# Two layers of a transformer block on one core: the first feed-forward groups as two pairs 512 columns wide, matmuls ordered by width, smaller first weight pieces

## The chip, the core and the metric

The kernel runs on one core of a Trainium2 chip. The time is the device time of one execution in microseconds (us); lower is better. Matrix products run on TensorE (PE), whose weight loads have a row of their own in the profile (PEld). VectorE (DVE), ScalarE (ACT) and GpSimd (POOL) do the elementwise work; SyncE (SP) issues nearly all DMAs.

## The reference

Two layers over 256 tokens of 1024 features. A mixer with three branches (a gated linear attention, a gated MLP over chunks, a softmax attention) ends in a residual and a layer norm. Then comes the part that the change is mostly about:

```python
x = layer_norm(DEEPNORM_ALPHA * x + mix, ln1_g[l], ln1_b[l])
ff = jnp.square(jax.nn.relu(x @ w_ff1[l])) @ w_ff2[l]      # 1024 -> 4096 -> 1024
x = layer_norm(DEEPNORM_ALPHA * x + ff, ln2_g[l], ln2_b[l])
```

All arrays are float32.

## The kernel before

**Precision.** TensorE multiplies in the type fp32r. Each float32 operand is split into a part `hi` (a cast on ScalarE) and a rest `lo` (a subtraction on VectorE); a product is the sum of hi·hi, hi·lo and lo·hi. The activations lie transposed, as `hi` and `lo` of 1024 features by 256 tokens, the two side by side so that `both` is one operand of 512 columns.

**Weights.** They come from memory in pieces of 1024 columns by 128 partitions (512 KB) into four raw buffers. `split_hi` makes `whi` (line 115) and `split_lo` makes `wlo` (line 120); each has 9 buffers (`SPLIT_BUFS`). The raw buffer is free once `wlo` is made, and then the next DMA is issued.

**Units.** The program is a list of units, each a stretch of matmuls (`pe`) that uses one or a few weight pieces, with work behind it (`post`). A planner at the end of the function fixes at which unit each piece is split: at most `LEAD` = 7 units ahead of its use, at most two pieces in one unit, and not before the piece that held the same buffer was used for the last time. The main loop then does the following for each unit, in this order, and each engine executes its instructions in the order in which they are written:

```python
        advance()      # next step of every generator in `side`
        splits(i)
        u.pe()
        if u.post:
            u.post()
```

Work that has to wait a while is put into `side` as a generator; each `yield` in it lets one more unit's matmuls go ahead of it.

**Three forms of matmul.** `acc_s` (line 287) has tokens as the stationary operand and weights as the moving one, 256 or 512 columns wide; its result has tokens on the partitions. `acc_w` (line 263) is the reverse, 256 wide. `acc_wide` (line 275) is the reverse with `both` as the moving operand: for each k one wide matmul (whi by `both`, 512 columns) and one narrow (wlo by `hi`, 256 columns), in turn.

**The feed-forward.** The 4096 hidden features are 16 groups of 256. Groups 3 to 15 are made by `ff1_units` with `acc_wide`: 2 units of 16 matmuls each, and no transpose is needed. The first three groups, the head, are made by `acc_s` for the first 128 tokens and then for the second, so that they can begin before the layer norm of the second 128 tokens is done: 6 units of 24 matmuls of 256 columns. Behind each, ScalarE does Relu (line 910) and Square (911) on the 128x256 result, TensorE transposes it in two pieces (919), and ScalarE and VectorE make `h` hi and lo (922, 923). The generator `tr` has two yields between Square and the transposes. `ff2_units(j)` multiplies group j by the second matrix, two units of 12 matmuls of 512 columns each, and alternates with `ff1_units(j + 3)`; the last three groups go into `out_units` (6 pieces).

**The layer norm** (`residual_norm`) of the second 128 tokens transposes its result (line 214, tile pT) at the start of the third unit after its own last one; line 216 casts it to `hi` and line 217 makes `lo`.

**The start.** `first_units` makes two products of 512 columns each (pSv, pSgv) over k = 0 to 7. Its pieces are 512 columns for k = 0 (two of them) and 1024 columns for k = 1 to 7; x comes in four pieces (k = 0; 1; 2 and 3; 4 to 7) that are split in `split_x` (lines 983, 984).

Of the kernel before, what the change touches and what calls it, by code (L numbers as in the profile page):

```python
# [9 lines left out]
F32 = mybir.dt.float32  # L10
# [4 lines left out]
OP = mybir.AluOpType  # L15
# [21 lines left out]
LEAD = 7  # L37
# [17 lines left out]
def block_kernel(ctx, tc, ins, out):  # L55
# [209 lines left out]
    def acc_wide(o, p, x, cs, k0, start, stop):  # L265


        hi, both = x[0], x[2]
        n = p.shape[0]
        for i in range(n):  # L270
            k = k0 + i
            tr = [(o, p.hi[:, i, cs], both[:, k, :]), (o[:, :256], p.lo[:, i, cs], hi[:, k, :])]
            last = stop and i == n - 1
            for j, (d, w, a) in enumerate(tr[::-1] if last else tr):
                nc.tensor.matmul(d, w, a, start=start and i == 0 and j == 0, stop=last and j == 1)  # L275
# [27 lines left out]
    def build_layer(l, xT):  # L303
# [285 lines left out]
        def first_units():  # L589

            blocks = [(0, piece(w_in[:, 0:1, C_V:C_V + 512], 1, 512)), (0, piece(w_in[:, 0:1, C_GV:C_GV + 512], 1, 512))]
            blocks += [(k, piece(w_in[:, k:k + 1, C_V:C_V + 1024], 1, 1024)) for k in range(1, 8)]
            heads = {0: 0, 2: 1, 3: 2, 5: 3}
            for n, (k, p) in enumerate(blocks):
# [3 lines left out]
                def pe(k=k, p=p, n=n):  # L598
                    for i, nm in enumerate(("v", "gv")):
                        if n < 2 and i != n:  # L600
                            continue
                        c0 = i * 512 if n > 1 else 0
                        for t in range(NT):
                            if k == 0:
                                st["ps_" + nm, t] = pbank("ps", "pS" + nm)
                            o, ts, cs = st["ps_" + nm, t], slice(t * 128, (t + 1) * 128), slice(c0, c0 + 512)
                            nc.tensor.matmul(o, xT()[0][:, k, ts], p.hi[:, 0, cs], start=k == 0, stop=False)
                            nc.tensor.matmul(o, xT()[1][:, k, ts], p.hi[:, 0, cs], start=False, stop=False)
                    for i, nm in enumerate(("v", "gv")):
                        if n < 2 and i != n:  # L610
                            continue
                        c0 = i * 512 if n > 1 else 0
# [279 lines left out]
        NS = 3  # L892
# [6 lines left out]
        fb = [w_pieces(wf1, j * 256, 256) for j in range(NS)]  # L899
        for t in range(NT):  # L900
            for j in range(NS):
                def pe(j=j, t=t):
                    p = st["pf", j, t] = pbank("pw", "pF")
                    for k in range(8):
                        acc_s(p[:, :256], fb[j][k // 4], k % 4, x1T(), k, t, slice(0, 256), k == 0, k == 7)

                def post(j=j, t=t):
                    def tr():
                        r = sbt("SP" if j % 2 else "PT", 384, "fr", bufs=2)[:, :256]
                        nc.scalar.activation(r, st["pf", j, t][:, :256], AF.Relu)  # L910
                        nc.scalar.activation(r, r, AF.Square)
                        yield
                        yield
                        if t == 0:
                            new_h(j)
                        hi, lo = st["h", j]
                        p = pbank("pw", "pFT")
                        for i in range(2):
                            nc.tensor.transpose(p[:, i * 128:(i + 1) * 128], r[:, i * 128:(i + 1) * 128], ident)
                        ts = slice(t * 128, (t + 1) * 128)  # L920
                        pv = v3(p[:, :256], 2)
                        nc.scalar.copy(hi[:, :, ts], pv)
                        nc.vector.tensor_tensor(lo[:, :, ts], pv, hi[:, :, ts].bitcast(F32), op=OP.subtract)
# [67 lines left out]
    units[3].start = sts[0]["params"]  # L991
# [23 lines left out]
    for n, p in enumerate(pieces):  # L1015
        free = max(q.last for q in pieces[:n - SPLIT_BUFS + 1]) + 1 if n >= SPLIT_BUFS else -LEAD
        s = max(prev + 1, free, p.first - (LEAD if n > 8 else 1))
# [5 lines left out]
        lo_at.setdefault(max(min(s + 1, p.first), s, -1) if n > 8 else max(s, -1), []).append(p)  # L1023
# [31 lines left out]
    for n, c in ((0, 0), (2, 1), (3, 2), (5, 3)):  # L1055
        load_more(n)
        load_xT(c)
# [56 lines left out]
```

## Time and profile before

| | us |
|---|---|
| median of 3 runs (lowest, highest) | 872.27 (872.25, 872.44) |
| the profiled execution, whole | 872.83 |
| its span, first to last instruction | 871.1 |
| TensorE busy | 860.2 (99% of the span) |
| VectorE busy | 617.7 (71%) |
| ScalarE busy | 468.0 (54%) |
| TensorE's share of the chain that ended last | 92% |

The span is the time from the first instruction to the last. The chain that ended last is followed back from the last instruction, at each step to what it waited for. A busy TensorE is not one at its peak: ends of matmuls are modelled and overlap, so rates are read from starts and from counts in a stretch.

### The profile page before, as it was taken

Reading aid. Unit: us, or ns where it says so; the run is one execution under the profiler, and the core shown is the slowest. Engines: PE = TensorE matmul, PEld = TensorE weight load, DVE = VectorE, ACT = ScalarE, POOL = GpSimd, SP = SyncE. Lnnn points to the kernel's source line nnn. Section 1 sums busy time; section 2 is a strip of 40 time slices with the busy share of each in tenths; the row PEclk is TensorE's granted clock in tenths of the full one; section 3 lists DMA queues with packets and bytes.
Section 4 is the critical chain, followed back from the end, with each engine's and each line's share of the span. In section 5 each row is a group of like instructions: output and inputs, shape, how many; then the busy total and the mean of one; then the engine's idle time right before and its main releaser. Section 6 shows DMA issues by size and latency. Waiting matters only on the chain.

```text
span 871.1 us, 13093 instructions
## 1 busy us (share of the span) xinstructions
PE 860.2 (99%) x5020; PEld 751.4 (86%) x5020; DVE 617.7 (71%) x949; ACT 468.0 (54%) x768; POOL 59.5 (7%) x73
## 2 busy tenths in 40 slices
PE   9999999999999999999999999999999999999996
PEld 7898887889989888888889898878898988888885
DVE  6779798666796666666777767958667856666665
ACT  6657663567445544445454756645744555444440
POOL 0010000102400000000000100010042000000001
PEclk9999999999999999999999999999999999999999
DMA  9577665346566655556655765544467465555531
GB/s 324 201 220 214 198 218 151 115 148 191 189 198 212 217 190 186 190 191 209 216 172 170 218 198 165 171 120 146 151 217 229 147 224 193 193 194 194 194 121 48
DMA packets 118718, 162.10 MB, mean 186 GB/s; under 512 B 5472, under 2 KB 100480, under 8 KB 118656
## 3 DMA queue, kind: packets, MB, share of 16 engines
q1 hardware_dynamic: 118512, 161.15, 57.8%
q8 instruction: 39, 0.64, 0.3%
q14 instruction: 23, 0.19, 0.1%
q10 hardware_dynamic: 144, 0.13, 0.0%
HBM read 160.21 MB, written 1.05 MB: 185 GB/s over the span
## 4 chain that ended last, share of the span: by engine, by line
PE 92%; DVE 3%; DMA 2%; ACT 1%; issue 1%; SPq 0%; DVEq 0%; ACTq 0%
PE acc L287 25%; PE pW L275 25%; PE pF L275 17%; PE pB L263 8%; PE pF L287 4%; PE pSmv L287 3%; DVE wlo L120 1%; PE pGG L287 1%; PE pSgv L287 1%; PE pSv L287 1%; PE pkv L457 1%; DMA xraw<-in_xT_dram 1%; DMA inv<-in_rope_inv_dram 1%; PE po L481 1%; PE pT L214 1%
## 5 line engine op out<-in xcount | busy, mean ns | idle before, releaser
L115 ACT CAST whi<-wraw 128x1024 fp32r<-128x1024 f32 (+1 forms) x281 | 283.3, 1039 | 132.2 <-DMA wraw<-in_w_ff_dram 63.2
L120 DVE TENSOR_TENSOR wlo<-wraw,whi 128x1024 fp32r<-128x1024 f32 (+1 forms) x281 | 334.7, 1226 | 18.1 <-ACT whi L115 17.8
L275 PE MATMUL pW<-actT,whi 128*128 128x512 f32 x704 | 248.3, 401 | 0.0
L275 PE MATMUL pW<-actT,wlo 128*128 128x256 f32 x704 | 183.3, 281 | 0.0
L287 PE MATMUL acc<-whi,h 128*128 128x512 f32 x512 | 163.4, 391 | 0.0
L275 PEld LDWEIGHTS pW<-actT,whi 128*128 128x128 f32 x704 | 128.1, 188 | 24.4
L275 PE MATMUL pF<-actT,whi 128*128 128x512 f32 x416 | 146.7, 397 | 0.0
L275 PEld LDWEIGHTS pW<-actT,wlo 128*128 128x128 f32 x704 | 132.9, 189 | 7.3 <-DVE wlo L120 0.2
L287 PEld LDWEIGHTS acc<-whi,h 128*128 128x128 f32 x512 | 96.2, 188 | 19.0
L275 PE MATMUL pF<-actT,wlo 128*128 128x256 f32 x416 | 108.4, 281 | 0.0
L287 PE MATMUL acc<-wlo,h 128*128 128x512 f32 x256 | 99.8, 390 | 0.0
L279 DVE TENSOR_TENSOR fr<-pF,fr 128x256 f32<-128x256 f32 x52 | 21.9, 424 | 102.0 <-ACT fr L278 102.0
L275 PEld LDWEIGHTS pF<-actT,whi 128*128 128x128 f32 x416 | 76.5, 188 | 15.4
L275 PEld LDWEIGHTS pF<-actT,wlo 128*128 128x128 f32 x416 | 78.5, 189 | 4.4
L287 PEld LDWEIGHTS acc<-wlo,h 128*128 128x128 f32 x256 | 48.1, 188 | 10.0
L278 ACT COPY fr<-pF 128x256 f32<-128x256 f32 x52 | 19.1, 372 | 59.4 <-PE pF L275 59.4
L209 POOL TENSOR_TENSOR mvar<-mvar,halfc 128x1 f32<-128x1 f32 x12 | 10.8, 904 | 443.1 <-DVE mvar L208 443.1
L287 PE MATMUL acc<-whi,actT 128*128 128x512 f32 x128 | 40.3, 391 | 0.0
L287 PE MATMUL pF<-whi,actT 128*128 128x256 f32 x192 | 36.6, 287 | 0.0
L279 DVE TENSOR_TENSOR gates<-pW,gates 128x256 f32<-128x256 f32 x48 | 19.5, 421 | 17.8 <-ACT gates L278 17.4
L278 ACT COPY gates<-pW 128x256 f32<-128x256 f32 x48 | 16.9, 370 | 27.3 <-PE pW L275 27.3
L946 ACT CAST h<-fr 128x256 fp32r<-128x256 f32 x52 | 19.3, 407 | 21.5 <-DVE fr L945 21.5
(234 smaller groups left out, 1238.6 us busy)
## 6 DMA issues: line engine op xcount, KB each, us to landing
wraw<-in_w_ff_dram SPq DMA_DIRECT2D x128, 512.0 KB, 4.9
wraw<-in_w_in_dram SPq DMA_DIRECT2D x104, 512.0 KB, 4.3
wraw<-in_w_branch_dram SPq DMA_DIRECT2D x24, 512.0 KB, 4.3
wraw<-in_w_out_dram SPq DMA_DIRECT2D x16, 512.0 KB, 3.3
wearly<-in_w_in_dram SPq DMA_DIRECT2D x7, 512.0 KB, 9.4
wraw<-in_w_in_dram SPq DMA_DIRECT2D x6, 396.0 KB, 4.4
lng<-in_ln_g_dram SPq DMA_DIRECT2D x4, 512.0 KB, 5.4
lnb<-in_ln_b_dram SPq DMA_DIRECT2D x4, 512.0 KB, 7.3
```

The lines of the kernel that those rows point to most:

```text
L115: nc.scalar.copy(p.hi, p.raw)
L120: nc.vector.tensor_tensor(p.lo, p.raw, p.hi.bitcast(F32), op=OP.subtract)
L209: nc.gpsimd.tensor_tensor(dst, dst, half_c.to_broadcast([128, n]) if n > 1 else half_c, op=OP.pow)
L214: nc.tensor.transpose(p[:, k * 128:(k + 1) * 128], src[:, (half * 4 + k) * 128:(half * 4 + k + 1) * 128], ident)
L263: nc.tensor.matmul(o, w, a, start=start and i == 0 and j == 0, stop=stop and i == n - 1 and j == 2)
L275: nc.tensor.matmul(d, w, a, start=start and i == 0 and j == 0, stop=last and j == 1)
L278: nc.scalar.copy(dst, p[:, 256:])
L279: nc.vector.tensor_tensor(dst, p[:, :256], dst, op=OP.add)
L287: nc.tensor.matmul(o, a, w, start=start and j == 0, stop=stop and j == 2)
L457: nc.tensor.matmul(p[:, h * 128:(h + 1) * 128], kT4[rows, t, h, :], v4[rows, t, h, :], start=True, stop=True)
L481: nc.tensor.matmul(p[r, c], at4[:, t, h, r], v4[:, t, h, :], start=first and r.start == 0, stop=True)
L946: nc.scalar.copy(hi[:, i], rr[i])
```

## The change

Three things. **The head** covers four groups instead of three, in two pairs: 4 units of 24 matmuls of 512 columns; Relu and Square are 128x512, four transposes follow each unit, and `tr` has one yield instead of two before them. Its weights come in eight pieces instead of six. Twelve groups instead of 13 are left to `ff1_units`, and the last `out_units` of a layer has 8 pieces instead of 6. **The order in `acc_wide`**: for each unit and result tile first four wide matmuls, then four narrow ones, or the reverse where the sum ends. **The first pieces**: four of 512 columns (k = 0 and 1), then 1024 columns for k = 2 to 7.

```diff
@@ acc_wide
-        for i in range(n):
-            k = k0 + i
-            tr = [(o, p.hi[:, i, cs], both[:, k, :]), (o[:, :256], p.lo[:, i, cs], hi[:, k, :])]
-            last = stop and i == n - 1
-            for j, (d, w, a) in enumerate(tr[::-1] if last else tr):
-                nc.tensor.matmul(d, w, a, start=start and i == 0 and j == 0, stop=last and j == 1)
+        wide = [(o, p.hi[:, i, cs], both[:, k0 + i, :]) for i in range(n)]
+        narrow = [(o[:, :256], p.lo[:, i, cs], hi[:, k0 + i, :]) for i in range(n)]
+        tr = narrow + wide if stop else wide + narrow
+        for j, (d, w, a) in enumerate(tr):
+            nc.tensor.matmul(d, w, a, start=start and j == 0, stop=stop and j == len(tr) - 1)
@@ first_units
-            blocks = [(0, piece(w_in[:, 0:1, C_V:C_V + 512], 1, 512)), (0, piece(w_in[:, 0:1, C_GV:C_GV + 512], 1, 512))]
-            blocks += [(k, piece(w_in[:, k:k + 1, C_V:C_V + 1024], 1, 1024)) for k in range(1, 8)]
-            heads = {0: 0, 2: 1, 3: 2, 5: 3}
+            blocks = [(k, piece(w_in[:, k:k + 1, c:c + 512], 1, 512)) for c in (C_V, C_GV) for k in (0, 1)]
+            blocks += [(k, piece(w_in[:, k:k + 1, C_V:C_V + 1024], 1, 1024)) for k in range(2, 8)]
+            heads = {0: 0, 1: 1, 4: 2, 6: 3}
@@ build_layer, the feed-forward
-        NS = 3
+        NS = 4
...
-        fb = [w_pieces(wf1, j * 256, 256) for j in range(NS)]
+        fb = [w_pieces(wf1, j * 512, 512, 8, 2) for j in range(NS // 2)]
         for t in range(NT):
-            for j in range(NS):
+            for j in range(NS // 2):
                 def pe(j=j, t=t):
                     p = st["pf", j, t] = pbank("pw", "pF")
                     for k in range(8):
-                        acc_s(p[:, :256], fb[j][k // 4], k % 4, x1T(), k, t, slice(0, 256), k == 0, k == 7)
+                        acc_s(p, fb[j][k // 2], k % 2, x1T(), k, t, slice(0, 512), k == 0, k == 7)

                 def post(j=j, t=t):
                     def tr():
-                        r = sbt("SP" if j % 2 else "PT", 384, "fr", bufs=2)[:, :256]
-                        nc.scalar.activation(r, st["pf", j, t][:, :256], AF.Relu)
+                        if t == 0:
+                            st["fr", j] = sbt(("Rk", "Rgg")[j], 1024, "fr")
+                        r = st["fr", j][:, t * 512:(t + 1) * 512]
+                        nc.scalar.activation(r, st["pf", j, t], AF.Relu)
                         nc.scalar.activation(r, r, AF.Square)
                         yield
-                        yield
-                        if t == 0:
-                            new_h(j)
-                        hi, lo = st["h", j]
                         p = pbank("pw", "pFT")
-                        for i in range(2):
+                        for i in range(4):
                             nc.tensor.transpose(p[:, i * 128:(i + 1) * 128], r[:, i * 128:(i + 1) * 128], ident)
                         ts = slice(t * 128, (t + 1) * 128)
-                        pv = v3(p[:, :256], 2)
-                        nc.scalar.copy(hi[:, :, ts], pv)
-                        nc.vector.tensor_tensor(lo[:, :, ts], pv, hi[:, :, ts].bitcast(F32), op=OP.subtract)
+                        pv = v3(p, 4)
+                        for i in range(2):
+                            if t == 0:
+                                new_h(2 * j + i)
+                            hi, lo = st["h", 2 * j + i]
+                            nc.scalar.copy(hi[:, :, ts], pv[:, 2 * i:2 * i + 2])
+                            nc.vector.tensor_tensor(lo[:, :, ts], pv[:, 2 * i:2 * i + 2], hi[:, :, ts].bitcast(F32), op=OP.subtract)
```

How the instructions stand is shown at three places. First TensorE in the first layer's head, behind the second head unit of the kernel before (`pF` are head matmuls, `pFT` the transposes of a head result, `pT` those of the layer norm, `fr` is what Relu and Square wrote, and a name in brackets is an engine that the row waits for):

```order
L287 MATMUL pF<-wlo,actT 128x256
L287 MATMUL pF<-whi,actT 128x256
L214 MATMUL pT<-ident,xr_67 128x128 [waits DVE_49,PE_49]
L214 MATMUL pT<-ident,xr_67 128x128 x3
L214 MATMUL pT<-ident,xr_67 128x128 [waits DVE_49,PE_49]
L214 MATMUL pT<-ident,xr_67 128x128 x3
L919 MATMUL pFT<-ident,fr 128x128 [waits Activation_49]
L919 MATMUL pFT<-ident,fr 128x128
L287 MATMUL pF<-whi,actT 128x256 [waits Activation_49]
```

The changed kernel, behind its first head unit:

```order
L286 MATMUL pF<-wlo,actT 128x512
L286 MATMUL pF<-whi,actT 128x512
L916 MATMUL pFT<-ident,fr 128x128 [waits Activation_49]
L916 MATMUL pFT<-ident,fr 128x128 x3
L286 MATMUL pF<-whi,actT 128x512 [waits PE_49]
L286 MATMUL pF<-wlo,actT 128x512 [waits DVE_49]
```

and behind the second, where the layer norm's transposes stand too:

```order
L286 MATMUL pF<-whi,actT 128x512
L214 MATMUL pT<-ident,xr_67 128x128 [waits PE_49]
L214 MATMUL pT<-ident,xr_67 128x128 x7
L916 MATMUL pFT<-ident,fr 128x128 [waits PE_49,Activation_49]
L916 MATMUL pFT<-ident,fr 128x128 x3
L286 MATMUL pF<-whi,actT 128x512 [waits Activation_49]
```

The two transposes before belong to the first head unit, whose 24 matmuls lie a whole unit back; the four now belong to the unit whose last matmul stands directly above them.

Second, VectorE at the same head, from the end of the second layer norm on; before:

```order
L242 SCALAR_TENSOR_TENSOR xr_67<-xr_67,mvar,lnb 128x512 [waits DVE_49]
L120 TENSOR_TENSOR wlo<-wraw,whi 128x1024 [waits DMAHW0_49,Activation_49]
L120 TENSOR_TENSOR wlo<-wraw,whi 128x1024 [waits DMAHW1_49,Activation_49]
L217 TENSOR_TENSOR actT<-pT,actT 128x4x128 [waits Activation_49] x2
L923 TENSOR_TENSOR h<-pFT,h 128x2x128 [waits Activation_49]
L120 TENSOR_TENSOR wlo<-wraw,whi 128x1024 [waits DMAHW2_49]
```

and in the changed kernel:

```order
L242 SCALAR_TENSOR_TENSOR xr_67<-xr_67,mvar,lnb 128x512 [waits DVE_49]
L924 TENSOR_TENSOR h<-pFT,h 128x2x128 [waits Activation_49] x2
L120 TENSOR_TENSOR wlo<-wraw,whi 128x1024 [waits DMAHW1_49]
L120 TENSOR_TENSOR wlo<-wraw,whi 128x1024 [waits DMAHW2_49]
L120 TENSOR_TENSOR wlo<-wraw,whi 128x1024 [waits DMAHW3_49,Activation_49]
L217 TENSOR_TENSOR actT<-pT,actT 128x4x128 [waits Activation_49] x2
```

The three `wlo` here are those of the second head unit's second, third and fourth piece; they now stand behind the two `h` rows, which come from the transposes at that unit's start.

Third, VectorE at the program's start, before:

```order
L120 TENSOR_TENSOR wlo<-wearly,whi 128x512 [waits DMAHW1_49,Activation_49]
L120 TENSOR_TENSOR wlo<-wearly,whi 128x512 [waits DMAHW2_49,Activation_49]
L984 TENSOR_TENSOR actT<-xraw,actT 128x256 [waits DMAHW3_49,Activation_49]
L984 TENSOR_TENSOR actT<-xraw,actT 128x2x256 [waits DMAHW5_49,Activation_49]
L120 TENSOR_TENSOR wlo<-wearly,whi 128x1024 [waits DMAHW4_49]
```

and in the changed kernel:

```order
L985 TENSOR_TENSOR actT<-xraw,actT 128x256 [waits DMAHW2_49,Activation_49]
L120 TENSOR_TENSOR wlo<-wearly,whi 128x512 [waits DMAHW1_49]
L120 TENSOR_TENSOR wlo<-wearly,whi 128x512 [waits DMAHW3_49,Activation_49]
L120 TENSOR_TENSOR wlo<-wearly,whi 128x512 [waits DMAHW4_49,Activation_49]
L120 TENSOR_TENSOR wlo<-wearly,whi 128x512 [waits DMAHW5_49,Activation_49]
L985 TENSOR_TENSOR actT<-xraw,actT 128x2x256 [waits DMAHW6_49,Activation_49]
```

The `wlo` of k = 1 stood behind the split of x for k = 2 and 3 (128x2x256); both halves of it now stand ahead of that split.

## Rows read from the trace of the kernel before

**Rows 1.** Page of the profile: busy time (part 1), granted TensorE clock (part 2).

```profile
PE 860.2 (99%) x5020; PEld 751.4 (86%) x5020; DVE 617.7 (71%) x949; ACT 468.0 (54%) x768; POOL 59.5 (7%) x73
...
PEclk9999999999999999999999999999999999999999
```

**Rows 2.** Who waited for whom on TensorE, whole span: total, times, longest (us).

```profile
PE pSv L614 <- DVE wlo L120: 1.1, 1, 1.1
```

**Rows 3.** Chain of work that ended last: start us, length us, what, count.

```profile
255.17 5.75 PE pF L287 x48
...
280.15 5.63 PE pF L275 x32
285.78 5.44 PE acc L287 x24
```

**Rows 4.** Timeline of TensorE between two head units: start, length, engine, line, operation.

```profile
264.61 0.28 PE L287 MATMUL pF<-whi,actT 128*128 128x256 f32 x1
264.73 0.38 PE L919 MATMUL pFT<-ident,fr 128*128 128x128 f32 x2
...
265.06 0.28 PE L287 MATMUL pF<-wlo,actT 128*128 128x256 f32 x1
```

**Rows 5.** Timeline of ScalarE behind the unit that ends in rows 4.

```profile
264.93 0.38 ACT L910 ACTIVATE fr<-pF 128x256 f32<-128x256 f32 x1 [0.95 <-PE pF L287]
265.34 0.42 ACT L911 ACTIVATE fr<-fr 128x256 f32<-128x256 f32 x1
```

**Rows 6.** Timeline of ScalarE, one instruction 512 columns wide.

```profile
53.71 0.62 ACT L373 CAST bh<-vs 128x512 fp32r<-128x512 f32 x1 [1.34 <-DVE vs L372]
```

**Rows 7.** Timeline of VectorE at the first head.

```profile
252.93 1.27 DVE L217 TENSOR_TENSOR actT<-pT,actT 128x512 fp32r<-128x512 f32 x2
...
264.26 0.41 DVE L923 TENSOR_TENSOR h<-pFT,h 128x256 fp32r<-128x256 f32 x1
264.59 1.22 DVE L120 TENSOR_TENSOR wlo<-wraw,whi 128x1024 fp32r<-128x1024 f32 x1
```

**Rows 8.** Timeline of TensorE, eight transposes and the second matmul behind them.

```profile
432.11 1.03 PE L214 MATMUL pT<-ident,xr 128*128 128x128 f32 x8
...
433.21 0.39 PE L287 MATMUL acc<-wlo,h 128*128 128x512 f32 x1
```

**Rows 9.** Timeline of TensorE, where two transposes waited.

```profile
74.74 0.39 PE L740 MATMUL plr<-ident,lrs 128*16 128x128 f32 x2 [0.82 <-DVE gates L279]
74.88 0.48 PE L275 MATMUL pW<-actT,whi 128*128 128x512 f32 x1
```

**Rows 10.** Timeline of TensorE, 512-column matmuls after a long run of 256.

```profile
232.33 0.40 PE L287 MATMUL acc<-whi,actT 128*128 128x512 f32 x1
...
233.49 0.62 PE L287 MATMUL acc<-whi,actT 128*128 128x512 f32 x2
```

**Rows 11.** Chain of work that ended last, at the program's start.

```profile
9.99 0.69 DVE actT L984
10.68 1.15 DVE wlo L120
...
11.87 0.73 PE pSv L614 x2
```

**Rows 12.** Timeline of ScalarE at the start: weight cast of the third k.

```profile
10.71 1.04 ACT L115 CAST whi<-wearly 128x1024 fp32r<-128x1024 f32 x1 [0.76 <-DMA wearly<-in_w_in_dram]
```

**Rows 13.** Timeline of TensorE at the start: before and after its first stall.

```profile
5.47 0.63 PE L608 MATMUL pSv<-whi,actT 128*128 128x512 f32 x1
5.89 0.63 PE L607 MATMUL pSv<-whi,actT 128*128 128x512 f32 x1
...
12.43 0.63 PE L614 MATMUL pSgv<-wlo,actT 128*128 128x512 f32 x2
12.90 0.40 PE L607 MATMUL pSv<-whi,actT 128*128 128x512 f32 x1
```

**Rows 14.** Page, DMA issues (part 6): count, KB each, median us to landing.

```profile
wraw<-in_w_ff_dram SPq DMA_DIRECT2D x128, 512.0 KB, 4.9
```

More of the change, by code (lines that the diff above doesn't have):

```diff
@@ L599, in pe @@
                     for i, nm in enumerate(("v", "gv")):
-                        if n < 2 and i != n:
+                        if n < 4 and i != n // 2:
                             continue
-                        c0 = i * 512 if n > 1 else 0
+                        c0 = i * 512 if n > 3 else 0
                         for t in range(NT):
@@ L609, in pe @@
                     for i, nm in enumerate(("v", "gv")):
-                        if n < 2 and i != n:
+                        if n < 4 and i != n // 2:
                             continue
-                        c0 = i * 512 if n > 1 else 0
+                        c0 = i * 512 if n > 3 else 0
                         for t in range(NT):
@@ L990, in block_kernel @@
         sts.append(s)
-    units[3].start = sts[0]["params"]
+    units[5].start = sts[0]["params"]
     units[6].start = lambda: side.append(late_consts())
@@ L1016, in block_kernel @@
         free = max(q.last for q in pieces[:n - SPLIT_BUFS + 1]) + 1 if n >= SPLIT_BUFS else -LEAD
-        s = max(prev + 1, free, p.first - (LEAD if n > 8 else 1))
+        s = max(prev + 1, free, p.first - (LEAD if n > 9 else 1))
         if count < 2 and max(prev, free) == prev and (p.first - s < 3 or p.first - s < LEAD - 1 and prev >= extra + 2):
@@ L1022, in block_kernel @@
         hi_at.setdefault(max(s, -1), []).append(p)
-        lo_at.setdefault(max(min(s + 1, p.first), s, -1) if n > 8 else max(s, -1), []).append(p)
+        lo_at.setdefault(max(min(s + 1, p.first), s, -1) if n > 9 else max(s, -1), []).append(p)
     loaded = [0]
@@ L1053, in advance @@
                 side.remove(g)
-    for n, c in ((0, 0), (2, 1), (3, 2), (5, 3)):
+    for n, c in ((0, 0), (1, 1), (4, 2), (6, 3)):
         load_more(n)
```

## Prediction

> **What bounds the kernel now.** I read the page first. TensorE is busy in 860.2 of 871.1 us, and its granted clock is at the full level in all 40 slices [rows 1]; so what it waits and what each matmul costs set the time. Next, who waited for whom on TensorE: the largest entry is one wait of 1.1 us at the start [rows 2], so the other engines and the DMAs are hidden nearly everywhere. Last, the chain that ended last gives rates, by counts and lengths: head matmuls of 256 columns take 5.75/48 = 0.1198 us each, matmuls of 512 columns 5.44/24 = 0.2267 us, and a wide and a narrow one of the alternating form 5.63/16 = 0.3519 us together [rows 3]. At 2.4 GHz 256 columns last 0.1067 us and 512 last 0.2133 us, so each matmul carries about 13 ns of its own, whatever its width, and the alternating pair costs 0.3519 - 0.2267 - 0.1198 = 5.4 ns more than its two members do in runs of their own. A change can therefore gain little by fewer or better ordered matmuls, and lose much by a single new wait.
>
> **The change part by part.** The profiled execution took 872.83 us, its span 871.1 and 1.7 around it; the median of the runs is 0.56 lower. I work out differences in us and add them to the median.
>
> *1. Fewer, wider matmuls.* Before, a layer's first feed-forward product is 144 matmuls of 256 columns and 13 groups of 32: 144 x 0.1198 + 13 x 5.63 = 90.4. Now it is 96 of 512 columns and 12 groups: 96 x 0.2267 + 12 x 5.63 = 89.3. Gain 1.1 per layer, **-2.2** in all. This lies on the path, as all of TensorE's work does. The rows have both widths, so the term has narrow bounds, -1.8 to -2.6. The Trainium skill, page "TensorE: Matmul & The Clock Gate", section "Back-to-back issue gap", gives a warm matmul N/2.4 + 2.5 ns, a fixed part of 2.5 ns instead of my 13. By that rule 160 fewer matmuls would give 0.4 instead of 2.2, and the sum would come out 1.8 higher; the rows show 0.2267 where the rule has 0.2157.
>
> *2. Transposes of the head.* Two transposes lengthen the stretch by 265.06 - 264.73 - 0.12 = 0.21 [rows 4]; eight by 433.21 - 432.11 - 0.23 = 0.87 [rows 8], so 0.11 each. Before there are 12 per layer and now 16: **+0.9** in two layers.
>
> *3. Waits in the head.* This is the large term. With one yield fewer, the four transposes of a head unit stand directly behind that unit's last matmul, ahead of the next unit, and TensorE takes its instructions in order. They wait until ScalarE has done Relu and Square on the result of the matmul that has just ended. Before, a whole unit lay between. The price comes from ScalarE's rows: Relu starts 0.32 after the start of the last matmul (264.61 to 264.93), 0.04 after its modelled end, and Square 0.03 after Relu ends [rows 4, 5]. At 512 columns the matmul lasts 0.39 [rows 8], and I take 0.62 for each ScalarE instruction from a 512-wide one [rows 6]. With 0.05 for the handover to TensorE, as from VectorE at the start (10.68 + 1.15 = 11.83 to 11.87) [rows 11], the transposes start 0.39 + 0.04 + 0.62 + 0.04 + 0.62 + 0.05 = 1.76 after the start of the last matmul. Without a wait it would be 0.23. So 1.53 are lost, behind the first, third and fourth unit in full. Behind the second, the layer norm's eight transposes (0.87) fill part of it: 0.65 remain. But the third unit is also the first that uses the result of these eight: its casts come behind Square on ScalarE, and its `lo` on VectorE, 0.64 for each half [rows 7], comes third; I take 0.25 for both. Behind the first unit comes one more: the second unit needs `wlo` of its second piece at its eighth matmul, and on VectorE that stands behind the two `h` rows of the transposes just done. From the last transpose's start: 0.27 to its end, 0.04, a cast of 0.38 like Relu's [rows 5], 0.04, two `h` of 0.33 and one `wlo` of 1.22 [rows 7] make 2.6, plus 0.05; TensorE arrives after 0.03 + 0.31 + 6 x 0.2267 = 1.7. That is 1.0 lost. The later pieces of that unit follow at 1.2 each against 6 x 0.2267 = 1.36, in time. The sum per layer is 3 x 1.53 + 0.9 + 1.0 = 6.5, in all **+13.0**. No row shows this wait itself. The lower bound takes ScalarE at the 0.4 of its 256-wide rows (0.44 less per unit) and no wait for `wlo`: 3.7 per layer, 7.5 in all. The upper bound puts one cast of a weight piece (1.04) [rows 12] ahead of Relu at two units of a layer, as can happen where a DMA lands late: 17.
>
> *4. The order of wide and narrow.* If the extra 5.4 ns of a pair went altogether, 1088 pairs (16 x (44 + 24): 44 such groups outside the feed-forward, 24 in it) would give -5.9. But the extra seems to belong to the passage from narrow to wide: after a long run of 256, five matmuls of 512 took 233.49 - 232.33 = 1.16, where five take 1.134 in their own run [rows 10], so a passage costs 26 ns and fades within five. Grouped, 16 pairs have three such passages, 78 ns at most, against 16 x 5.4 = 86 now; four wide ones pay nearer 20, and I take 27 ns of gain for 16 pairs. That is **-1.8**, with bounds -5.9 and +1.5. That narrow ones now come first where a sum ends asks for `wlo` 0.23 earlier; the planner splits it a unit ahead, so nothing.
>
> *5. The start.* TensorE's one long wait, 1.1 us up to 11.87, came because `wlo` of k = 1 (10.68) came behind the split of x for k = 2 (9.99) [rows 2, 11]. Now the former no longer stands behind the latter. The gain ends where k = 2 begins, which needs its own weights, cast by 10.71 + 1.04 = 11.75 [rows 12], against 12.90 for it before [rows 13]: 1.15 at most, 0 at least. I take **-0.9**, since one DMA more is issued ahead.
>
> *6. Fewer pieces ahead.* Eight pieces live through the head, so only one of nine buffers is left, and at the first `ff2` unit the splits are some two units ahead instead of six. VectorE is busy 71% of the span [rows 1], so of the 11.07 of a group of four units [rows 3] some 3 are free, two more `wlo`, and the lead comes back within two groups. Nothing, but see the rivals. The longer tail of 8 pieces has the same matmuls in another order: nothing.
>
> The sum is -2.2 + 0.9 + 13.0 - 1.8 - 0.9 = **+9.0**, to 872.3 + 9.0 = **881.3 us**, slower by 1.0%. About 0.2% (1.7 us) is what a measurement of this kernel can tell from no change.
>
> **The rivals.** *A, faster: the new wait is covered.* TensorE would have to run the next head unit's matmuls while the transposes wait, or ScalarE would have to be done as soon as the matmul ends. Then terms 1, 2, 4 and 5 are left: -4.0, 868.3. It decides from 2.2 us on: the head's waits must sum to less than that for the kernel to be faster by over 0.2%. Against it: two transposes at 74.74 waited 0.82 for VectorE, and the wide matmul behind them started only after them, at 74.88 [rows 9].
>
> *B, slower still: the feed-forward behind the head runs short of pieces.* Weights that come one load and split late (4.9 to land [rows 14], 1.04 and 1.22, less two units of 2.75) stop TensorE for some 1.7 per layer: +3.4, 884.7. For it speaks the smaller lead, against it VectorE's room in step 6.
>
> *C, much slower: the waits lower TensorE's clock.* At the start matmuls of 512 columns came every 0.42 at the lower level [rows 13], 0.2 more each. If six matmuls, one piece's share of a head unit, ran so behind each of ten waits, +12 would come, 893. Against it: behind the wait of 1.1 us they came every 0.235 (12.43 to 12.90) [rows 2, 13]. The Trainium skill, same page, section "A second HAM failure mode: psum-queue depth-cycling", says that brief idling of TensorE between groups of matmuls can send its clock back and forth; by that rule this case would come, and no row here shows it.
>
> *D, no change within 0.2%: the order gives its full 5.9 and the head's waits lie at their lower bound.* Then -2.2 + 0.9 - 5.9 - 1.2 + 7.5 = -0.9, 871.4. Each bound is possible; both at once is not likely.
>
> **How the numbers follow.** My forecast has 0.73, A 0.08, B 0.10, C 0.03, D 0.06. The range is the forecast's: with terms 3, 4 and 5 two thirds of the way to their low bounds it ends at 881.3 - 3.7 - 2.7 - 0.2 = 874.7, to their high ones at 881.3 + 2.8 + 2.2 + 0.6 = 886.9, and B lies inside. It leaves out A, C and D and a little of the forecast's ends, 0.2 in all. Faster by over 0.2%: A, 0.08. Within: D and the forecast's low end, 0.07. Slower: the rest, 0.85.
>
> **What would show it.** In the changed profile, TensorE waits on Square (line 912) ahead of the transposes (line 916), some 1.5 us, at three places per layer, and shorter once; one wait of about 1 us on `wlo` in the second head unit; the pair of a wide and a narrow matmul near 0.350; the second product's k = 2 starting near 12.0 instead of 12.90. Wrong would be: no such waits in the head, a granted clock below full there, or waits of TensorE on weights later in the feed-forward.

## The result and the profile after

The changed kernel took **885.26 us** (median of 4 runs, 884.72 to 885.63), the kernel before 872.36 beside it (4 runs, 872.25 to 872.77): a ratio of 1.0144, 95% interval 1.013 to 1.0157. It is slower by 12.9 us; the prediction said 881.3, with a range of 875 to 887.

The page of the changed kernel, busy time and granted clock:

```profile
PE 860.9 (97%) x4868; PEld 742.4 (84%) x4868; DVE 614.8 (70%) x942; ACT 468.0 (53%) x757; POOL 59.9 (7%) x73
...
PEclk9999999999999999999999999999999999999999
```

The clock is as before, and TensorE's busy time too [rows 1], while the span grew from 871.1 to 883.1 us. So the time went into idle time of TensorE. Who waited for whom on TensorE (us in total, times, longest):

```profile
PE pFT L916 <- ACT fr L912: 9.0, 8, 1.4
PE pF L286 <- DVE wlo L120: 2.6, 2, 1.3
PE warm L136 <- DVE warmt L131: 1.1, 1, 1.1
PE pSv L606 <- ACT whi L115: 1.0, 1, 1.0
PE pSgv L286 <- DVE wlo L120: 0.5, 1, 0.5
PE plr L739 <- DVE gates L278: 0.2, 1, 0.2
```

The first two entries are new: eight waits of the head's transposes on Square, four in each layer, and two of a head unit on `wlo`. `pSgv` is new too; it lies at the boundary of the layers. (`warm` stands at the start, ahead of the first product, and `plr` are the two transposes of [rows 9].)

The chain that ended last gives the time by stage. Of the changed kernel: the first head matmul of each layer, one group of the alternating form, one of the second product, and the first row of the last layer norm:

```profile
253.65 5.45 PE pF L286 x24
...
291.24 5.58 PE pF L274 x32
296.82 5.46 PE acc L286 x24
...
688.83 5.45 PE pF L286 x24
...
875.29 0.70 DVE xr L228
```

and of the kernel before, beside its 255.17 of [rows 3]:

```profile
683.34 5.75 PE pF L287 x48
...
863.19 0.70 DVE xr L228
```

Three stages come from these: up to the first head (255.17 before, 253.65 now), from head to head (428.17, 435.18), from the second head to the last norm (179.85, 186.46). The changes are -1.52, +7.01 and +6.61, together +12.1. That is also the difference of the two profiled executions (884.9 less 872.83); the medians differ by 0.8 more, since the one lies 0.36 below its median and the other 0.47 above. Nearly all of it is in the two feed-forwards. TensorE in the first layer there, behind the first head unit:

```profile
258.70 0.39 PE L286 MATMUL pF<-whi,actT 128*128 128x512 f32 x1
260.44 0.66 PE L916 MATMUL pFT<-ident,fr 128*128 128x128 f32 x4 [1.35 <-ACT fr L912]
260.85 0.48 PE L286 MATMUL pF<-whi,actT 128*128 128x512 f32 x1
...
262.10 0.63 PE L286 MATMUL pF<-whi,actT 128*128 128x512 f32 x2
264.02 0.50 PE L286 MATMUL pF<-wlo,actT 128*128 128x512 f32 x1 [1.29 <-DVE wlo L120]
```

and behind the second, where the layer norm's transposes fill a part:

```profile
268.03 1.03 PE L214 MATMUL pT<-ident,xr 128*128 128x128 f32 x8
269.54 0.66 PE L916 MATMUL pFT<-ident,fr 128*128 128x128 f32 x4 [0.47 <-ACT fr L912]
270.01 0.50 PE L286 MATMUL pF<-whi,actT 128*128 128x512 f32 x1
270.35 0.40 PE L286 MATMUL pF<-wlo,actT 128*128 128x512 f32 x1
270.74 0.73 PE L286 MATMUL pF<-whi,actT 128*128 128x512 f32 x2
271.31 0.40 PE L286 MATMUL pF<-wlo,actT 128*128 128x512 f32 x1
```

The transposes start 1.74 after the last matmul (258.70 to 260.44), where they started 0.12 behind it before [rows 4]. Read from starts, 1.74 less the 0.227 of a matmul, 1.51 are lost. The same 1.51 stands behind the third and fourth unit and at all three places of the second layer; behind the second unit it is 0.64 (268.03 to 269.54, less 0.87 for the eight transposes). The stop on `wlo` costs 1.46: the second of the two matmuls at 262.10 started at 262.33, and from there to 264.02 are 1.69, less 0.227. Last, 0.16 are lost at the start of the third unit (270.35 to 270.74, less 0.227), on the norm's `actT`. A layer's waits sum to 3 x 1.51 + 0.64 + 1.46 + 0.16 = 6.8.

### The profile page after: what moved, and what is told of

Its sections match the earlier page's. It is cut to its first block, busy times and chain, and to the rows that moved or that the text cites. A ratio compares the mean times of both kernels' runs of the same rounds, so it can differ in the third digit from the quotient of the medians.

```text
span 883.1 us, 12754 instructions
## 1 busy us (share of the span) xinstructions
PE 860.9 (97%) x4868; PEld 742.4 (84%) x4868; DVE 614.8 (70%) x942; ACT 468.0 (53%) x757; POOL 59.9 (7%) x73
## 4 chain that ended last, share of the span: by engine, by line
PE 89%; DVE 4%; ACT 3%; DMA 3%; issue 1%; SPq 0%; DVEq 0%; ACTq 0%
PE pW L274 25%; PE acc L286 24%; PE pF L274 15%; PE pB L263 8%; PE pF L286 5%; PE pSmv L286 3%; DVE wlo L120 2%; PE pGG L286 1%; DMA wraw<-in_w_in_dram 1%; DMA wearly<-in_w_in_dram 1%; PE pSgv L286 1%; PE pkv L456 1%; DMA posi<-in_positions_dram 1%; PE po L480 1%; PE pSv L286 1%
## 5 line engine op out<-in xcount | busy, mean ns | idle before, releaser
L115 ACT CAST whi<-wraw 128x1024 fp32r<-128x1024 f32 (+2 forms) x282 | 284.0, 1038 | 144.0 <-DMA wraw<-in_w_ff_dram 70.4
L120 DVE TENSOR_TENSOR wlo<-wraw,whi 128x1024 fp32r<-128x1024 f32 (+2 forms) x282 | 334.9, 1222 | 29.9 <-ACT whi L115 29.6
L274 PE MATMUL pW<-actT,whi 128*128 128x512 f32 x704 | 190.8, 397 | 0.0
L274 PEld LDWEIGHTS pW<-actT,wlo 128*128 128x128 f32 x704 | 102.5, 189 | 11.6
L274 PE MATMUL pW<-actT,wlo 128*128 128x256 f32 x704 | 107.3, 282 | 0.0
L274 PE MATMUL pF<-actT,whi 128*128 128x512 f32 x384 | 104.2, 393 | 0.0
L274 PEld LDWEIGHTS pF<-actT,wlo 128*128 128x128 f32 x384 | 55.4, 188 | 6.0
L274 PE MATMUL pF<-actT,wlo 128*128 128x256 f32 x384 | 57.0, 280 | 0.0
L286 PE MATMUL pF<-whi,actT 128*128 128x512 f32 x128 | 41.7, 397 | 0.0
L286 PEld LDWEIGHTS pF<-whi,actT 128*128 128x128 f32 x128 | 23.9, 188 | 5.7 <-DVE actT L217 0.9
```

What stands on the lines that cost most here:

```text
L115: nc.scalar.copy(p.hi, p.raw)
L120: nc.vector.tensor_tensor(p.lo, p.raw, p.hi.bitcast(F32), op=OP.subtract)
L274: nc.tensor.matmul(d, w, a, start=start and j == 0, stop=stop and j == len(tr) - 1)
L286: nc.tensor.matmul(o, a, w, start=start and j == 0, stop=stop and j == 2)
```

## The experiments

Each ratio is to the kernel before on the same chip (its medians there were 872.82 to 873.26), with its 95% interval. The stages are those above, from each trace's chain; they show tenths that the medians can't.

| kernel | ratio | to first head | head to head | second head to end |
|---|---|---|---|---|
| before | 1 | 255.17 | 428.17 | 179.85 |
| changed | 1.0144 (1.013 to 1.0157) | 253.65 | 435.18 | 186.46 |
| two yields | 0.9993 (0.9984 to 1.0002) | 253.73 | 429.64 | 180.53 |
| order alone | 0.9983 (0.9974 to 0.9992) | 255.36 | 427.52 | 179.50 |
| first pieces alone | 0.9983 (0.9974 to 0.9992) | 253.70 | 428.16 | 179.85 |
| head alone | 1.0176 (1.0158 to 1.0193) | 255.44 | 436.64 | 186.80 |
| no Square | 1.0077 (1.0064 to 1.0089) | 253.25 | 432.70 | 183.83 |
| splits first | 1.0095 (1.0082 to 1.0109) | 253.07 | 433.59 | 184.86 |
| tail of six | 1.0128 (1.0114 to 1.0141) | 254.21 | 434.44 | 186.45 |
| order and first pieces | 0.9972 (0.9962 to 0.9982) | 253.11 | 427.53 | 179.50 |
| the same, again | 0.9964 (0.9951 to 0.9976) | 253.11 | 427.54 | 179.51 |
| three parts mended | 0.9990 (0.9981 to 0.9999) | 253.50 | 428.60 | 180.60 |
| early norm | 0.9978 (0.9969 to 0.9987) | 254.10 | 428.15 | 180.10 |
| `lo` first | 0.9960 (0.9946 to 0.9973) | 253.19 | 427.20 | 179.19 |

**Theory and rival.** My theory: the head's transposes wait for Relu and Square, since one yield puts them directly behind their own unit. The rival: the wider head with its eight pieces costs the time itself.

### Two yields in the changed kernel

```diff
                         nc.scalar.activation(r, r, AF.Square)
                         yield
+                        yield
```

> The changed kernel with the second yield of `tr` put back, so that a whole head unit again stands between a result and its transposes; everything else as changed. My theory, the waits behind Relu and Square: the three waits of 1.5 us, the one of 0.64 and most of the 1.46 on `wlo` go from each layer (6.8 measured per layer, up to 13.6 in all), some 0.5 per layer may come back where the last head unit's result is now transposed later and its `h` is needed soon. So 885.3 - 12.5 to 13.6, that is 871.5 to 873, about equal to the kernel before. Rival, the wider head itself or its eight weight pieces that live through it cost the time (pieces late, buffers short): TensorE then waits on weights instead, and the time stays at 880 to 885.

The ratio fell to 0.9993, 1.5% below the changed kernel's: the theory holds, the rival falls. TensorE's waits behind the start, by the view of who waited for whom:

```profile
PE pF L286 <- ACT actT L216: 1.0, 2, 0.5
PE pSgv L286 <- DVE wlo L120: 0.8, 1, 0.8
```

Not one wait on Square is left. But the stages show that a layer takes 1.0 more than in the kernel with order and first pieces alone (180.53 to 179.50), and 1.34 more than in the last kernel below, whose wide head doesn't wait (179.19). The third unit waits for the norm's cast, 0.67 by starts (1.11 less 0.44 for four transposes), and 0.16 for its `lo`; a `wlo` behind the head costs 0.35. TensorE at the third unit:

```profile
265.46 0.60 PE L917 MATMUL pFT<-ident,fr 128*128 128x128 f32 x4
266.57 0.50 PE L286 MATMUL pF<-whi,actT 128*128 128x512 f32 x1 [0.51 <-ACT actT L216]
```

### Each part alone

Order alone:

```diff
...
+        wide = [(o, p.hi[:, i, cs], both[:, k0 + i, :]) for i in range(n)]
+        narrow = [(o[:, :256], p.lo[:, i, cs], hi[:, k0 + i, :]) for i in range(n)]
+        tr = narrow + wide if stop else wide + narrow
...
```

> The kernel before with nothing but the grouped order of wide and narrow matmuls in `acc_wide` (1100 or so pairs now, one feed-forward group per layer more than in the changed kernel). Theory one, the extra of an alternating pair belongs to the passage from narrow to wide and the grouped order keeps it at most in part: the changed kernel's rates (5.58 instead of 5.63 for 32, 28.07 instead of 28.16 for 160) give -1.0 to -1.3, so 871.1 to 871.4; my term 4 said -1.8 to -2.0, 870.4. Rival, the extra goes altogether, 1120 x 5.4 ns = -6.0, 866.3, and something else in the changed kernel hides it. Other rival, narrow ones first where a sum ends ask earlier for `wlo` and cost what the order gives: 872.3.

First pieces alone:

```diff
...
+            blocks = [(k, piece(w_in[:, k:k + 1, c:c + 512], 1, 512)) for c in (C_V, C_GV) for k in (0, 1)]
+            blocks += [(k, piece(w_in[:, k:k + 1, C_V:C_V + 1024], 1, 1024)) for k in range(2, 8)]
...
```

> The kernel before with nothing but the smaller first pieces (four of 512 columns for k = 0 and 1, and the planner's bounds that count them). Theory: the gain at the start, 1.4 us by the time 75 us into the span of the changed kernel, is a gain of this part alone and nothing behind it is in a position to eat it, since TensorE is never idle for a DMA later: 872.35 - 1.4 = 870.9 to 871.4. Rival: the weights of the next products then come late by the same amount and the gain is given back within the first layer: 872.3.

Head alone:

```diff
-        NS = 3
+        NS = 4
...
-            for j in range(NS):
+            for j in range(NS // 2):
...
```

> The kernel before with nothing but the head in two pairs of 512 columns (one yield, four transposes per unit, eight pieces in the tail). If the parts add up: the changed kernel is 12.9 above the kernel before, the order gives about -1.1 and the first pieces -1.4 there, so this kernel is 12.9 + 2.5 = +15.4, 887.7; by my prediction's terms 1 to 3 it would be +11.7, 884.0. Rival, the parts do not add (the grouped order costs something in the head, or the start's gain is given back): 885.3 or below.

The ratios give -1.5, -1.5 (each 0.7 to 2.3) and +15.4 us (13.8 to 16.8), and these add up to +12.4; the changed kernel has +12.6 by its ratio. In the traces the third stage adds up to a hundredth (-0.35, 0 and +6.95 for +6.61); from head to head the head alone costs 0.8 more than the rest predicts, and its wait on `pSgv` is 1.3 where the changed kernel has 0.5. So two parts each gain, and the head loses ten times as much. The order's gain is -0.65 from head to head and -0.35 behind the second head, the theory's size: in two layers 1.3, a fifth of the 5.9 that 5.4 ns for every pair would give. The first pieces gain 1.47 up to the first head and nothing is given back later.

### No Square

```diff
                         nc.scalar.activation(r, st["pf", j, t], AF.Relu)
-                        nc.scalar.activation(r, r, AF.Square)
```

> The changed kernel without the Square behind each head result: the hidden features of the four head groups are relu instead of its square, nothing else is left out. Square takes 0.63 of ScalarE per head unit. My theory, the transposes wait for the chain of Relu and Square and handover: each wait gets shorter by 0.63 to 0.66, so the three full ones come to 0.87, the one of 0.64 goes, and the wait on `wlo` in the second head unit loses nothing to 0.6 (what comes behind starts earlier by the same). Per layer 3 x 0.65 + 0.64 = 2.6, so 5.2 to 6.2 in all: 885.3 - 5.2 to 6.2 = 879 to 880. Rival, the waits are set by something else (the weight pieces, or a fixed cost of turning to transposes): no change, 885.

ScalarE and TensorE behind the first unit of the first layer:

```profile
258.72 0.60 ACT L911 ACTIVATE fr<-pF 128x512 f32<-128x512 f32 x1 [5.51 <-PE pF L286]
```

```profile
258.30 0.39 PE L286 MATMUL pF<-whi,actT 128*128 128x512 f32 x1
259.38 0.66 PE L915 MATMUL pFT<-ident,fr 128*128 128x128 f32 x4 [0.69 <-ACT fr L911]
```

The transposes now start 1.08 after the last matmul instead of 1.74: 0.66 less for Square's 0.63. Behind the second unit the wait is gone. A layer is shorter by 186.46 - 183.83 = 2.63, and 3 x 0.66 + 0.64 = 2.62. The dose fits to a hundredth, so the four waits follow ScalarE's chain one for one: of the 1.08 that are left, 0.42 pass until Relu starts, 0.60 are Relu, and 0.06 the handover. The wait on `wlo` stayed (1.47 by starts): what it hangs on begins and ends earlier by the same.

### Splits first in the second head unit

```diff
+        st["second_head"] = first_ff - 2 * (NS // 2) + 1
...
-        advance()
-        splits(i)
+        if i in [s["second_head"] for s in sts]:
+            splits(i)
+            advance()
+        else:
+            advance()
+            splits(i)
```

> The changed kernel with the weight splits written ahead of the transposes and `h` rows in the second head unit of each layer alone. Theory: the wait of 1.46 on `wlo` there comes from the three `wlo` that stand behind the two `h` rows on VectorE and their casts; with the splits ahead it goes, and the `h` rows, which nothing needs soon, wait instead: 1.46 x 2 = -2.9, 882.4. A cost may come instead: the casts of the pieces on ScalarE stand ahead of nothing urgent there, so at most some 0.3 back. Rival, the pieces themselves land or are cast too late there, whatever stands ahead: no change, 885.3.

The ratio is 0.5% lower, and a layer is shorter by 186.46 - 184.86 = 1.60. VectorE at that unit:

```profile
258.66 3.49 DVE L120 TENSOR_TENSOR wlo<-wraw,whi 128x1024 fp32r<-128x1024 f32 x3
262.07 0.42 DVE L924 TENSOR_TENSOR h<-pFT,h 128x256 fp32r<-128x256 f32 x1
```

The three `wlo` begin as soon as the layer norm is done, at 258.66, and TensorE has no wait on `wlo` in the head any more. In the changed kernel they stood behind the `h` rows (VectorE; then ScalarE):

```profile
261.54 0.42 DVE L924 TENSOR_TENSOR h<-pFT,h 128x256 fp32r<-128x256 f32 x1 [2.21 <-ACT h L923]
262.41 0.42 DVE L924 TENSOR_TENSOR h<-pFT,h 128x256 fp32r<-128x256 f32 x1 [0.44 <-ACT h L923]
262.75 3.48 DVE L120 TENSOR_TENSOR wlo<-wraw,whi 128x1024 fp32r<-128x1024 f32 x3
```

```profile
261.13 0.37 ACT L923 CAST h<-pFT 128x256 fp32r<-128x256 f32 x1 [0.75 <-PE pFT L916]
262.00 0.37 ACT L923 CAST h<-pFT 128x256 fp32r<-128x256 f32 x1 [0.49 <-DVE h L924]
```

Here is why it was 1.46 and not the 1.0 of my sum: the second cast on ScalarE waited 0.49 for VectorE's first `h` row, and VectorE's second row then waited 0.44 for that cast. I had the two casts side by side with the rows. The 0.14 that a layer gained beyond 1.46 is mostly the next thing: the second matmul after that wait came 0.11 late in the changed kernel.

### A tail of six pieces

```diff
+        NT2 = 3
+        for j in range(NF - NS, NF - NT2):
+            ff2_units(j)
...
-        b2 = [piece(wf2[:, k:k + 1, :], 1, 1024) for k in range(2 * (NF - NS), 2 * NF)]
+        b2 = [piece(wf2[:, k:k + 1, :], 1, 1024) for k in range(2 * (NF - NT2), 2 * NF)]
...
```

> The changed kernel with six pieces instead of eight in the last stretch of each layer's feed-forward (its thirteenth group goes through `ff2_units` like the ones ahead of it). Theory: the wait of 0.6 at the boundary of the two layers, which the trace of the kernel before does not have, comes from the longer run of pieces that are split ahead of the casts that follow; with six it goes: -0.6, 884.7. Rival, the wait comes from the order of work in the next layer's start, -0: 885.3.

The ratio's interval overlaps the changed kernel's, so the times alone don't decide. The trace does: head to head is shorter by 0.74, of which the wait on `pSgv` is 0.62 by starts, and it is gone; the third stage is the same to 0.01, and the start is later by 0.56 (its wait on `plr`, long before the tail, is 0.9 instead of 0.2). In the changed kernel the wait looked so (TensorE; then VectorE):

```profile
452.17 0.50 PE L286 MATMUL pSgv<-wlo,actT 128*128 128x512 f32 x1 [0.45 <-DVE wlo L120]
```

```profile
446.10 3.48 DVE L120 TENSOR_TENSOR wlo<-wraw,whi 128x1024 fp32r<-128x1024 f32 x3
449.70 1.29 DVE L217 TENSOR_TENSOR actT<-pT,actT 128x512 fp32r<-128x512 f32 x2
450.90 2.54 DVE L120 TENSOR_TENSOR wlo<-wraw,whi 128x1024 fp32r<-128x1024 f32 x2
```

In both kernels a `wlo` of the next layer stands behind the norm's two `actT` rows; in the changed kernel three `wlo` stand ahead of these rows, in the kernel with six pieces two (2.35 from 447.12 on). That the longer tail makes it late is shown by its undoing; by which rule of the planner was not traced.

### Order and first pieces without the head

> The kernel before with the grouped order and the smaller first pieces, but its own head of three groups of 256 columns. Alone the two parts measured -1.3 and -1.4 (each with an interval about 0.8 wide on either side). If they add up: 872.35 - 2.6 = 869.7, faster than both kernels by 0.3%. If they act on the same slack: -1.4, 871.

> The kernel with the grouped order and the smaller first pieces alone, once more, on the same chip as the two that try to mend the head, so that they can be compared. As before: a ratio of 0.997 to the kernel before, 0.998 at most.

Both runs are faster than the kernel before, by 0.28% and 0.36%; the medians were 870.27 and 869.83 us. The two parts add up, and the second and third stage repeat to 0.01 us.

### Can the wide head be freed of its waits?

Three parts mended together (two yields, tail of six, splits first); then in addition the first norm's transposes one unit earlier and the splits first at the unit behind the head; then, at that unit, only one `wlo` ahead of the `h` rows. The edits of the second and the third, in part:

```diff
-        yield
+        if not early:
+            yield
         yield
         hi, lo, _ = dst()
...
+        elif i in [s["second_head"] + 3 for s in sts]:
+            for p in lo_at[i][:1]:
+                while taken[0] <= rank[id(p)]:
+                    take_lo()
+            advance()
+            splits(i)
...
```

> The changed kernel with three parts mended: two yields in `tr`, six pieces in the tail, and the splits written first in the second head unit. With two yields alone the trace still has per layer a wait of 0.67 on the layer norm's cast at the third head unit (and 0.16 on its second half), 0.35 on a `wlo` behind the head, and 0.94 at the boundary of the layers. The tail of six takes the 0.94 away, the splits nothing more: 0.94 less than with two yields, a ratio of 0.9993 - 0.0011 = 0.998, still 1 us above the kernel with the order and first pieces alone. Rival: the boundary's wait is not the tail's, 0.9993 as with two yields.

Head to head is shorter than with two yields by 1.04, as the tail predicts; behind the second head it is not (180.60 to 180.53). The interval of the ratio is too wide to tell 0.9990 from 0.998.

> The kernel just named, and in addition the transposes of the first layer norm one unit earlier, at the start of the second head unit, and the splits first at the unit behind the head too. Theory: what is left at the third head unit is the cast of the layer norm's transposes, which comes behind Relu and Square of a unit that is now twice as long; done a unit earlier it goes (0.67 + 0.16 per layer), and the splits first take the 0.35 away: 2 x 1.2 = -2.4 against the kernel just named, a ratio of 0.998 - 0.0027 = 0.9953, below the kernel with the order and first pieces alone by 1.3 us (the 1.1 per layer of fewer and wider matmuls, less 0.47 for transposes, now left over). Rival: done earlier the transposes wait for VectorE's last row of the norm (it ends 0.4 after that unit's start) or their `lo` rows push back the `wlo` of the second unit, and a new wait of up to 1 us per layer takes the place of the old: 0.997 to 0.998.

Less than half came. No wait on the norm is left, but a layer gained 0.45 to 0.50 instead of 1.2. ScalarE and TensorE behind the head, with the splits first there:

```profile
279.09 1.03 ACT L115 CAST whi<-wraw 128x1024 fp32r<-128x1024 f32 x1
280.02 0.36 ACT L925 CAST h<-pFT 128x256 fp32r<-128x256 f32 x1
```

```profile
279.32 0.40 PE L287 MATMUL acc<-whi,h 128*128 128x512 f32 x1
280.44 0.50 PE L287 MATMUL acc<-whi,h 128*128 128x512 f32 x1 [0.72 <-ACT h L925]
```

A weight cast of 1.03 got ahead of the `h` cast that the next matmul needs: 0.89 lost by starts, in place of the 0.35 on `wlo`. My expectation had looked at VectorE's queue alone.

> The kernel with the early norm, but at the unit behind the head only one `wlo` of VectorE is written ahead of the `h` rows, and the weight casts of ScalarE stay behind the `h` casts. In the kernel with the early norm a new wait of 0.89 per layer (with 0.11 of slow refill) has come there, of the first second-product unit on an `h` cast of ScalarE that stands behind Relu, Square and a weight cast of 1.03. Theory: that is the price of having put the splits ahead on both engines; with only the `wlo` ahead, neither the 0.89 nor the 0.35 that stood there earlier is left, the wide head has no wait any more, and it is faster by its fewer and wider matmuls (1.1 less 0.47 per layer): 2 x 1.0 = -2.0 against the early norm's 0.9978, a ratio of 0.9955, below the 0.9964 to 0.9972 of the kernel with order and first pieces alone. Rival: a unit of `ff2` behind the head needs its `h` within half a unit, and the wait stays in another form: 0.997 to 0.998.

The whole list of TensorE's waits, but for `warm` at the start, is now one line:

```profile
PE pSv L607 <- ACT whi L115: 1.2, 1, 1.2
```

The ratio is 0.9960, the median 869.72 us. It beats both kernels, but from order and first pieces alone (0.9972 and 0.9964) its ratio can't be told. The two stages behind the start can: 0.31 to 0.34 less in each, which is what fewer and wider matmuls, less the added transposes, are worth in a layer once nothing waits. The transposes of a head unit, without a wait:

```profile
264.73 0.39 PE L287 MATMUL pF<-whi,actT 128*128 128x512 f32 x1
264.96 0.60 PE L918 MATMUL pFT<-ident,fr 128*128 128x128 f32 x4
265.32 0.48 PE L287 MATMUL pF<-whi,actT 128*128 128x512 f32 x1
265.63 0.40 PE L287 MATMUL pF<-wlo,actT 128*128 128x512 f32 x1
265.87 0.63 PE L287 MATMUL pF<-whi,actT 128*128 128x512 f32 x2
...
271.25 0.48 PE L287 MATMUL pF<-whi,actT 128*128 128x512 f32 x1
```

## Why the prediction was right, and where its terms were off

The mechanism was the one forecast, at the places forecast, and 885.26 lies in the range, near its upper end. The sum was +9.0 and is +12.1 in the traces, +12.9 in the medians; all terms but the start's missed on the slow side. Term by term, in both layers together:

| term | forecast | measured | from |
|---|---|---|---|
| 1 and 2, matmuls and transposes | -1.3 | -0.6 | `lo` first against order and first pieces |
| 3, waits in the head | +13.0 | +13.6 | starts in the changed trace |
| 3, slower restarts behind them | none | +1.0 | stages, 7.27 per layer less 6.79 |
| 4, order | -1.8 | -1.3 | order alone, 2 x 0.65 |
| 5, start | -0.9 | -1.2 | first stage, -1.52 less 0.3 of order |
| 6, pieces and tail | 0 | +0.7 | tail of six |

The measured column adds up to 12.2.

**Term 3** held in its parts: 1.51 for 1.53, 0.64 for 0.65, 0.16 for 0.25; the wait on `wlo` was 1.46 for 1.0, for the reason shown with the splits. What the step left out is that TensorE doesn't go on at full pace. From `lo` first to the changed kernel a layer grows by 186.46 - 179.19 = 7.27, the waits are 6.8 of it. The four transposes take 0.41 up to the next matmul's start behind a wait (260.44 to 260.85) and 0.36 without one (264.96 to 265.32), three times a layer; the second matmul behind the wait on `wlo` comes 0.11 late; and the start of the third unit loses some 0.2 beside its 0.16 (269.54 to 270.01 for four transposes, and 270.74 to 271.31 for two matmuls that take 0.47 in `lo` first). Together that is nearly the 0.48 between 7.27 and 6.79; 0.1 of it, at 270.01, may be a wait on the norm's cast rather than a restart.

**Terms 1 and 2**: in `lo` first a head unit without waits takes 5.93 from its first matmul (265.32) to that of the next unit (271.25); 24 x 0.2267 are 5.44 of it, so four transposes and the slower restart take 0.49. I had 0.44, which makes 0.4 over eight units. Another 0.1 is only a matter of division: measured among kernels with the grouped order, the two groups of 32 that the head replaces are worth 5.58 each, not 5.63 [rows 3]. The last 0.2 stay open. The page of the Trainium skill that the prediction weighed, "TensorE: Matmul & The Clock Gate", section "Back-to-back issue gap", gives its N/2.4 + 2.5 ns for an isolated matmul. An estimate of terms 1 and 2 by that rule is -0.4 + 0.9 = +0.5; the -0.6 measured lies on the rows' side, and the 24 matmuls of 5.45 us in the changed chain make 0.227 each where that rule has 0.216.

**Term 4** had the right mechanism as far as the rate goes (5.58 for 32 now, 0.349 a pair, as forecast). But the 24 matmuls of the feed-forward's second product take 5.46 instead of 5.44 [rows 3]; that comes with the order (5.46 in the chain with the order alone, 5.44 with the first pieces alone), and no run tells why. The 0.65 of head to head holds one feed-forward (0.35) and one mixer (0.3), and the first mixer is taken like the second: in the kernel with the order alone its 0.3 doesn't show, since `plr` waited 1.4 there for VectorE instead of 0.8 [rows 9]. **Term 5** gained more than its sum, and the same wait has a part in it: `plr` waited 0.2 in the changed kernel. Why is not shown: kernels with the new first pieces waited there from nothing to 0.9, the two others with the old ones 1.3 and 1.4, so the -1.2 is good to some tenths only (first pieces alone gained 1.47). The matmuls of k = 2 started at 12.35, between the 12.0 forecast and 12.90 [rows 13]; the first of them is of pSv, the first of the two products, and not of the second, as the prediction has it. They came later than forecast because ScalarE's cast stood behind a DMA that landed late, here ScalarE in the changed kernel:

```profile
11.25 1.04 ACT L115 CAST whi<-wearly 128x1024 fp32r<-128x1024 f32 x1 [0.71 <-DMA wearly<-in_w_in_dram]
```

**Term 6** failed at one sentence, "The longer tail of 8 pieces has the same matmuls in another order: nothing": the same work in another order put a `wlo` 0.62 late at the boundary of the layers. Its first half held: no wait on weights stands in the feed-forward behind the head. But that hangs on the order of work, and the step had not looked at it: with two yields a `wlo` behind the head came 0.35 late, standing behind two `h` rows on VectorE.

**The rivals.** A (the wait is covered) fell with the eight waits on Square; the kernel with two yields is that case, and it comes out at no change rather than at 868.3, since other waits come with it (1.34 per layer with their slow restarts, and 0.8 on `pSgv` at the boundary), and terms 1, 2 and 4 give 1.2 less than forecast. B would have been close in time, 884.7, but its place is empty: no wait on weights behind the head. C fell, with ten waits of up to 1.5 us. The granted clock, full in all 40 slices, can't show that by itself: from 4 to 6 us the profile gives 1.00 in both kernels too, where 512-column matmuls came every 0.42 [rows 13]. The starts can: behind a wait of 1.5 five matmuls took 1.25 (260.85 to 262.10), 0.25 each. The Trainium skill, same page, section "A second HAM failure mode: psum-queue depth-cycling", tells of a kernel whose brief idling between groups of matmuls sends the clock back and forth; the trace doesn't show that here, by the same starts. D fell with both of its bounds, the order's 1.3 and the waits' 13.6.

## What to carry to other kernels

Where one engine is busy nearly all the time and executes in order, an instruction that depends on work just finished costs the whole round trip through the other engine (here 1.74 us through two steps of ScalarE), as often as it stands there, less what other work stands between (0.64 instead of 1.51 were lost behind eight transposes); count who stands directly ahead of it, not how much work was saved. A part that gains 0.3 us per layer is easily bought with 7 us of waits. When moving work ahead on one engine to end a wait, look at the queue of every engine that the same piece of code issues to: a cast put ahead on ScalarE made a new wait while the row on VectorE ended the old.

## What the runs showed that was not expected

TensorE restarts slowly: a matmul takes 0.31 to the next start behind transposes (265.32 to 265.63) instead of 0.227, with or without a wait; and behind a wait in the middle of a unit the second matmul comes 0.11 late. The start varies between kernels that have the same first pieces: the first head began between 253.07 and 254.21, roughly the later the longer `plr` had waited (0.2 and less up to 253.25, 0.7 and 0.9 from 254.10 on), and the tail of six, which has the 0.9, changes nothing that stands ahead of that wait. The one program that was traced twice repeats in all three stages to 0.01. So between kernels, tenths should be read from stages behind the start.
